# The two MLP down projections computed by seven products of 2x2 blocks instead of eight

## The chip, the cores and the metric

The kernel is one program on one core of a Trainium2 chip. Its time is the device time of one execution in microseconds (us). TensorE (PE) multiplies 128x128 weight tiles with a moving operand and adds into eight PSUM banks; VectorE (DVE), ScalarE (ACT) and GpSimd (POOL) do the elementwise work; SyncE (SP) and others issue DMAs. The tensors are fp32. Products are taken in the fp32r format: an operand x is split into hi (x rounded to fp32r) and lo = x - hi, and a product becomes three matmuls: hi*hi, hi*lo and lo*hi.

## The reference

One inference step of a trunk of two layers on 1024 prompt tokens and 32 sample tokens (8 sequences of 4) with width 1024. Layer 0 has state-space mixers, layer 1 sparse attention. After each mixer stands the MLP, the place of the change; at the end a final RMSNorm.

```python
def sq_relu_mlp(xn, w_up, w_down):     # w_up 1024 x 4096, w_down 4096 x 1024
    h = jax.nn.relu(xn @ w_up)
    return (h * h) @ w_down
...
    hp = hp + sq_relu_mlp(rms_norm(hp, norm_mlp[layer]), w_up[layer], w_down[layer])
    hs = hs + sq_relu_mlp(rms_norm(hs, norm_mlp[layer]), w_up[layer], w_down[layer])
y_prompt = rms_norm(hp, norm_final)
y_sample = rms_norm(hs, norm_final)
```

## The kernel before

Activations lie with features on the partitions and the 1056 tokens along the free axis. Stages follow one another: layer 0's input projection and mixers, its output projection, MLP 0, the attention layer's input projection ("io", token tiles against weights), attention, its output projection, MLP 1 with the final norm.

The up projection of an MLP (`prod`, L1345 on) already uses seven products instead of eight, in Winograd's form: features of the input are taken as pairs of blocks, output features as pairs, tokens as two halves of 528. Weight sums (`sums`, L1310, POOL) and input differences (`b_sum`, L1225, POOL) are split into hi and lo (ACT cast, DVE subtraction: L1321 and L1322 for weights, L1215 and L1216 for inputs) and multiplied as tiles of 128x264 (L1355 to L1357). Each result is squared after relu on DVE (L1337), multiplied by the squared norm scale `r2` on POOL (L1338), and stored to the DRAM tensor `h_d`.

The down projection (`down`, L1391 on, `dense`, L369 on) goes over 8 groups G of 512 hidden features. Per group, four rows of `h_d` are loaded by SP and split (L330, L331), and weights arrive in units of 1024 columns through the shared weight queue (`w_load`, `w_split`: L306, L315, L316), which also prefetches the first units of the next stage. For each of 8 output blocks d and 3 token chunks of 352 there are 4 x 3 matmuls into a bank of four (`mm`); the result is added to Y in SBUF by DVE (L1400). In group 6 the residual is added, in group 7 each finished piece goes to `finish`: for layer 0 the sum of squares, the residual's store, and the hi and lo parts of the attention layer's input (`resid`, L1192 to L1197); for layer 1 the squares and, once a chunk of tokens is complete, the final norm (`norm4`, L2343 on) and the output's store.

What sets the order: a framework derives the semaphores from the tiles and places each engine's instructions by their order in the program, as far as their buffers are free; each engine then runs its queue in order. A tile's tag has a fixed number of buffers: "wh" 4, "w" 2, "h" 8 (of 512 columns), "sw" 3, "x" 5 in the MLP phase (one of them holds `r2`), "s" 25 (of 1056 columns).

Of the kernel before, what the change touches and what calls it, by code (L numbers as in the profile page):

```python
# [7 lines left out]
F32 = mybir.dt.float32  # L8
F32R = mybir.dt.float32r
# [94 lines left out]
def _prep(i):  # L104
# [90 lines left out]
def _build(ctx, nc, tc, ins, outs, dbg):  # L195
# [988 lines left out]
    def resid(d, c, src, g, xn, acc):  # L1184

        cc = slice(c * CH, (c + 1) * CH)
        if d == 0:
# [9 lines left out]
        V.scalar_tensor_tensor(lo, src, g, hi.bitcast(F32), op0=OP.mult, op1=OP.subtract)  # L1197

# [65 lines left out]
    def ob_unit(d):  # L1264
        def evac(c, p):
            a = ACC[d][:, c * CH:(c + 1) * CH]
            t = half(F32, "ot")
            V.tensor_tensor(t[:, :CH], p[:, :CH], rBs[:, c * CH:(c + 1) * CH], OP.mult)
            V.tensor_tensor(a, a, t[:, :CH], OP.add)
            resid_w(d, c, a, g_mlp[:, d:d + 1], WX1, acc1)  # L1270
# [22 lines left out]
    def mlp(l, W, acc, finish):  # L1293

        R, SF, SW = {}, {}, {}
        st = {"u": U_MLP[l], "H": {}, "Y": {}}
# [37 lines left out]
        def act(x, f, j, c):  # L1334
# [3 lines left out]
            nc.gpsimd.tensor_tensor(x, x, st["r2"][:, tok], OP.mult)  # L1338
# [46 lines left out]
        def h_load(G):  # L1385
            for k in range(4):
                t = xslot(F32, "hr")
                nc.sync.dma_start(t[:, :NT], h_d[l][4 * G + k])
                st["H"][k, G] = split1(t, "hh")

        def down(G, d):  # L1391
            def evac(c, p):
                cc = slice(c * CH, (c + 1) * CH)
                if G == 0:
                    if c == 0:
                        st["Y"][d] = slot(F32, "Y")
                    S.copy(st["Y"][d][:, cc], p[:, :CH])
                    return
                y = st["Y"][d]
                V.tensor_tensor(y[:, cc], y[:, cc], p[:, :CH], OP.add)  # L1400
                if G == 7:
                    finish(d, c, y)
                if G == 6:
                    res = half(F32, "res")
                    nc.sync.dma_start(res[:, :CH], res_d[2 * l][d][:, cc])
                    V.tensor_tensor(y[:, cc], y[:, cc], res[:, :CH], OP.add)
                if G == 7 and c == 2:
                    st["Y"][d] = None
            e = d % 2
            u = st["u"]  # L1410
            if e == 1:
                st["u"] += 1
            act = [st["H"][k, G] for k in range(4)]
            return dense(u, act, range(4), evac, off=512 * e, first=(e == 0), last=(e == 1))
# [993 lines left out]
```

## Time and profile before

| | |
|---|---|
| median of three runs | 3175.05 us (3171.71 to 3177.97) |
| the profiled execution | 3170.71 us, span 3168.8 us |
| PE, DVE, ACT, POOL busy in the span | 96%, 66%, 41%, 25% |
| mean granted clock of PE | 0.984 of full speed |
| DMA | 328.55 MB, 104 GB/s in the mean |

The span is what the profiler records between the first and the last instruction; the execution's own time has a little more around it. Busy times are shares of the span. A matmul's busy time is longer than the distance to the next one, since matmuls overlap; the number of matmuls in a stretch that PE fills says how far apart they are.

### The profile page before, as it was taken

Reading aid. Unit: us, or ns where it says so; the run is one execution under the profiler, and the core shown is the slowest. Engines: PE = TensorE matmul, PEld = TensorE weight load, DVE = VectorE, ACT = ScalarE, POOL = GpSimd, SP = SyncE. Lnnn points to the kernel's source line nnn. Section 1 sums busy time; section 2 is a strip of 40 time slices with the busy share of each in tenths; the row PEclk is TensorE's granted clock in tenths of the full one; section 3 lists DMA queues with packets and bytes.
Section 4 is the critical chain, followed back from the end, with each engine's and each line's share of the span. In section 5 each row is a group of like instructions: output and inputs, shape, how many; then the busy total and the mean of one; then the engine's idle time right before and its main releaser. Section 6 shows DMA issues by size and latency. Waiting matters only on the chain. (4 is left out here: it accounts for less than half of the span.)

```text
span 3168.8 us, 55263 instructions
## 1 busy us (share of the span) xinstructions
PE 3037.3 (96%) x21451; PEld 2871.4 (91%) x21451; DVE 2081.9 (66%) x4075; ACT 1290.5 (41%) x2575; POOL 784.0 (25%) x771
## 2 busy tenths in 40 slices
PE   7999998998999999999999989999999999999998
PEld 5999886898999999999999777777778999999998
DVE  4778787788766444466224777878776776644456
ACT  4223666434333321123236666666653333331112
POOL 0000000016666200001001344343333666510000
PEclk8999999999999999999999999999999999999999
DMA  5345453522333532228631122121143233353232
GB/s 185 94 128 156 113 131 120 165 85 94 106 107 106 173 101 96 67 87 247 163 92 57 18 67 59 23 61 41 21 119 118 95 106 109 113 174 99 78 93 80
DMA packets 219852, 328.55 MB, mean 104 GB/s; under 512 B 71283, under 2 KB 164694, under 8 KB 219526
## 3 DMA queue, kind: packets, MB, share of 16 engines
q1 hardware_dynamic: 189760, 264.03, 27.5%
q0 software_dynamic: 17728, 36.77, 4.7%
q10 hardware_dynamic: 12102, 24.22, 2.0%
q8 instruction: 169, 2.77, 0.4%
q14 instruction: 93, 0.76, 0.1%
HBM read 224.30 MB, written 92.22 MB: 100 GB/s over the span
## 5 line engine op out<-in xcount | busy, mean ns | idle before, releaser
L384 PE MATMUL mm<-hh,wh 128*128 128x352 f32 x1440 | 465.1, 323 | 0.2 <-ACT c L1363 0.2
L386 PE MATMUL mm<-hh,wh 128*128 128x352 f32 x1440 | 464.9, 323 | 0.0
L385 PE MATMUL mm<-hh,wh 128*128 128x352 f32 x1440 | 464.5, 323 | 0.0
L1400 DVE TENSOR_TENSOR Y<-Y,mm 128x352 f32<-128x352 f32 x336 | 173.8, 519 | 273.1 <-PE mm L386 272.3
L315 ACT CAST wh<-wr 128x1024 fp32r<-128x1024 f32 (+3 forms) x121 | 122.9, 1016 | 468.8 <-PE mm L385 453.4
L1355 PE MATMUL A<-xw,sw 128*128 128x264 f32 x1024 | 291.7, 286 | 2.3 <-ACT xw L1215 1.6
L1357 PE MATMUL A<-xw,sw 128*128 128x264 f32 x1024 | 292.4, 286 | 1.0 <-DVE sw L1322 1.0
L1356 PE MATMUL A<-xw,sw 128*128 128x264 f32 x1024 | 293.0, 286 | 0.1
L2124 POOL TENSOR_SCALAR P<-P,s,gates 128x640 f32<-128x640 f32 (+7 forms) x256 | 211.9, 841 | 277.1 <-DVE s L2120 229.0
L385 PEld LDWEIGHTS mm<-hh,wh 128*128 128x128 f32 x1440 | 271.2, 188 | 0.0
L384 PEld LDWEIGHTS mm<-hh,wh 128*128 128x128 f32 x1440 | 270.7, 188 | 0.4 <-ACT c L1363 0.4
L386 PEld LDWEIGHTS mm<-hh,wh 128*128 128x128 f32 x1440 | 270.9, 188 | 0.0
L1338 POOL TENSOR_TENSOR e<-e,r 128x264 f32<-128x264 f32 x192 | 196.6, 1030 | 225.1 <-DVE e L1337 221.6
L384 PE MATMUL mm<-xh,wh 128*128 128x352 f32 x672 | 224.5, 335 | 7.0 <-ACT xh L435 5.9
L385 PE MATMUL mm<-xl,wh 128*128 128x352 f32 x672 | 222.5, 331 | 5.2 <-DVE xl L436 5.2
L386 PE MATMUL mm<-xh,wh 128*128 128x352 f32 x672 | 221.7, 330 | 0.0
L2142 DVE TENSOR_TENSOR PT<-px,PT 128x512 fp32r<-128x512 f32 x264 | 176.8, 682 | 51.2 <-ACT PT L2141 50.6
L316 DVE TENSOR_TENSOR wh<-wr,wh 128x1024 fp32r<-128x1024 f32 (+3 forms) x121 | 143.8, 1188 | 100.1 <-ACT wh L315 100.1
L2166 PE MATMUL pv<-PT,vs 128*128 128x512 f32 x528 | 195.3, 438 | 11.6 <-ACT PT L2141 6.8
L2116 ACT ACTIVATE P<-sc,m 128x640 f32<-128x640 f32 (+7 forms) x256 | 180.1, 713 | 41.0 <-DVE m L2110 30.1
L1355 PEld LDWEIGHTS A<-xw,sw 128*128 128x128 f32 x1024 | 193.8, 190 | 2.9 <-ACT xw L1215 1.7
L1357 PEld LDWEIGHTS A<-xw,sw 128*128 128x128 f32 x1024 | 194.1, 190 | 1.4 <-DVE sw L1322 1.4
(631 smaller groups left out, 8305.6 us busy)
## 6 DMA issues: line engine op xcount, KB each, us to landing
hr<-h_d SPq DMA_DIRECT2D x64, 528.0 KB
wu<-i_w_up SPq DMA_DIRECT2D x64, 512.0 KB
wr<-i_w_dn SPq DMA_DIRECT2D x64, 512.0 KB
h_d<-e SPq DMA_DIRECT2D x192, 132.0 KB
wr<-i_w_in_e POOLq DMA_DIRECT2D x26, 512.0 KB, 4.1
h_d<-c SPq DMA_DIRECT2D x64, 132.0 KB
res<-res SPq DMA_DIRECT2D x48, 176.0 KB
csb<-cs_d SPq DMA_DIRECT2D x16, 512.0 KB
```

What stands on the lines that cost most here:

```text
L384: T.matmul(o, wh, xh, start=(j == 0), stop=False)
L385: T.matmul(o, wh, xl, start=False, stop=False)
L386: T.matmul(o, wl, xh, start=False, stop=(j == n - 1))
L1338: nc.gpsimd.tensor_tensor(x, x, st["r2"][:, tok], OP.mult)
L1355: T.matmul(o, a, xh, start=bool(first and q == 0), stop=False, skip_group_check=True)
L1356: T.matmul(o, a, xl, start=False, stop=False, skip_group_check=True)
L1357: T.matmul(o, b, xh, start=False, stop=(q == 3), skip_group_check=True)
L1400: V.tensor_tensor(y[:, cc], y[:, cc], p[:, :CH], OP.add)
L2116: S.activation(P, reg[:, h - h0], AF.Exp, bias=b["m"][:, h:h + 1], accum_out=b["s"][:, h:h + 1])
L2124: nc.gpsimd.tensor_scalar(P, P, b["s"][:, h:h + 1], GT[:, qb, gc:gc + 1], op0=OP.mult, op1=OP.mult)
L2142: V.tensor_tensor(lo, p, hi.bitcast(F32), OP.subtract)
L2166: T.matmul(PV[g, qb, i], v, t, start=(a == 0 and kb == 0 and k == 0), stop=False)
```

## The change

The down projection of both layers takes the hidden features, the output features and the tokens as 2x2 blocks and computes seven products p1 to p7 of blocks or of sums of blocks. In the diff, A are the weights and B the hidden activations: a step q (of 16) takes the pair of hidden rows 2q and 2q+1 and all 4 pairs of output blocks (dp). The products go one after the other (p1, p5, p6, p2, p4, p7, p3), each over all 16 steps, 24 matmuls of 264 columns a step, into all eight PSUM banks (`dn`). For every product the operands are loaded anew by SP (`a_load` 256 KB, `b_load` 264 KB); the sums TR (of B) and SR (of A) stay in SBUF and are altered in place by POOL from product to product (`ready`, `after`). `two_of` is the split. `ready` of a step stands two steps ahead of its matmuls in program order. `evac` adds the products into Y.

The product by `r2` moves from the up stage to the end: `done` takes a piece of 128x264 (32 pieces in all), multiplies it by `r2` (DVE), adds the residual (POOL), and calls `finish`, unless p3 is still to come for it. Two pieces are placed behind each step of p3. In layer 1, p3 is done in two passes over the token quarters (`last`), with its weight sum split already during p7 into `S4`, and the final norm is called between the steps (`hook4`). The prefetch of the first three weight units of the attention layer's input projection is held until MLP 0 is through. `w_dn` is laid out in memory as 64 blocks of 128x512.

```diff
-        a[f"w_dn{l}"] = np.stack([np.concatenate([_unit(wd[G * 512:(G + 1) * 512, d * 128:(d + 1) * 128])
-                                                  for d in (2 * e, 2 * e + 1)], 1) for G in range(8) for e in range(4)])
+        a[f"w_dn{l}"] = np.ascontiguousarray(wd.reshape(16, 2, 128, 4, 2, 128).transpose(4, 1, 0, 2, 3, 5).reshape(64, 128, 512))
...
-        return psum[-1][1].tile([128, 512], F32, name=f"{name}{cnt[0]}", tag="px", bufs={"att": 3, "up": 1}.get(psum[-1][2], 4))
+        return psum[-1][1].tile([128, 512], F32, name=f"{name}{cnt[0]}", tag="px", bufs={"att": 3, "up": 1}.get(psum[-1][2], 4)) if psum[-1][2] != "dn" else dn()
+    def dn():
+        cnt[0] += 1
+        return psum[-1][1].tile([128, 512], F32, name=f"dn{cnt[0]}", tag="dn", bufs=8)
...
-    U_MLP = [len(units), 0]
-    def mlp_units(l):
-        return [(ins[f"w_dn{l}"][j], 1024) for j in range(32)]
-    units += mlp_units(0)
...
-    U_MLP[1] = len(units)
-    units += mlp_units(1)
...
-    held = {U_MLP[l] + i for l in range(2) for i in range(2)}
+    held = {U_IO + i for i in range(3)}
...
+    seen = set()
+    def sq_add(acc, cc, src, key):
+        if (key, cc.start) not in seen:
+            seen.add((key, cc.start))
             S.activation(acc[:, cc], src, AF.Square)
         else:
-            t = half(F32, "sq")[:, :CH]
+            t = half(F32, "sq")[:, :cc.stop - cc.start]
             S.activation(t, src, AF.Square)
             V.tensor_tensor(acc[:, cc], acc[:, cc], t, OP.add)
-        if c == 0:
+    def resid(d, cc, src, g, xn, acc):
+        sq_add(acc, cc, src, "acc2")
+        if d not in xn:
             xn[d] = slot(F32R, "xn"), slot(F32R, "xn")
         hi, lo = (t[:, cc] for t in xn[d])
         S.activation(hi, src, AF.Copy, scale=g)
         V.scalar_tensor_tensor(lo, src, g, hi.bitcast(F32), op0=OP.mult, op1=OP.subtract)
...
-            nc.gpsimd.tensor_tensor(x, x, st["r2"][:, tok], OP.mult)
             nc.sync.dma_start(h_d[l][f][:, tok], x)
...
-        def h_load(G):
...
-        def down(G, d):
...
+        Y, TR, SR, S4, PS = {}, {}, {}, {}, {}
+        def a_load(i, k, q):
+            t = half(F32, "ar")
+            nc.sync.dma_start(t, ins[f"w_dn{l}"][(2 * i + k) * 16 + q])
+            return t
+        def b_load(k, j, q, second=False, o=0, n=HF):
+            t = wslot(F32, "br", "w", 2) if second else ptile(F32, "br", "sw", 3, 1024)
+            nc.sync.dma_start(t[:, :n], h_d[l][2 * q + k][:, j * HF + o:j * HF + o + n])
+            return t[:, :n]
+        def stay(Z, q, n):
+            if q % 2 == 0:
+                Z["t"] = slot(F32, "st")
+            Z[q] = Z["t"][:, q % 2 * n:(q % 2 + 1) * n]
+            return Z[q]
+        def two_of(x, t):
+            n = x.shape[-1]
+            hi, lo = t[:, :n], t[:, n:2 * n]
+            S.copy(hi, x)
+            V.tensor_tensor(lo, x, hi.bitcast(F32), OP.subtract)
+            return hi, lo
+        sub = lambda o, x, y: nc.gpsimd.tensor_tensor(o, x, y, OP.subtract)
+        wt = lambda: wslot(F32R, "sb", "wh", 4)
+        xt_ = lambda: xslot(F32R, "xb")
+        def ready(n, q):
+            if n == "p1":
+                a, x, b12 = a_load(0, 0, q), b_load(0, 0, q), b_load(0, 1, q, True)
+                sub(stay(TR, q, HF), b12, x)
+            elif n == "p5":
+                a21, a22 = a_load(1, 0, q), a_load(1, 1, q)
+                a = stay(SR, q, 512)
+                nc.gpsimd.tensor_tensor(a, a21, a22, OP.add)
+                x = TR[q]
+            elif n == "p6":
+                a, x = SR[q], TR[q]
+                sub(a, a, a_load(0, 0, q))
+            elif n == "p2":
+                a, x = a_load(0, 1, q), b_load(1, 0, q)
+            elif n == "p4":
+                a, b21 = a_load(1, 1, q), b_load(1, 0, q)
+                x = ptile(F32, "t4", "wr", 2, 1024)[:, :HF]
+                sub(x, b21, TR[q])
+            elif n == "p7":
+                a, x = half(F32, "s3"), TR[q]
+                sub(a, a_load(1, 1, q), SR[q])
+            else:
+                a, x = half(F32, "s4"), b_load(1, 1, q)
+                sub(a, a_load(0, 1, q), SR[q])
+            return two_of(a, wt()), two_of(x, xt_())
+        def after(n, q):
+            if n == "p5":
+                sub(TR[q], b_load(1, 1, q), TR[q])
+            elif n == "p4":
+                sub(TR[q], TR[q], b_load(0, 0, q, True))
+            elif n == "p7" and l:
+                sub(SR[q], a_load(0, 1, q), SR[q])
+                S4[q] = two_of(SR[q], slot(F32R, "s4"))
+        tok = lambda j, c: slice(j * HF + c * 264, j * HF + (c + 1) * 264)
+        res_ = lambda d, cc: res_d[2 * l][d][:, cc]
+        def scale_res(d, cc):
+            y, res = Y[d][:, cc], half(F32, "res")[:, :264]
+            nc.sync.dma_start(res, res_(d, cc))
+            V.tensor_tensor(y, y, st["r2"][:, cc], OP.mult)
+            nc.gpsimd.tensor_tensor(y, y, res, OP.add)
+        todo = []
+        def evac(n, dp, c, o):
+            d0, d1 = 2 * dp, 2 * dp + 1
+            if n in ("p1", "p5") and c == 0:
+                Y[d0 if n == "p1" else d1] = slot(F32, "Y")
+            y = lambda i, j: Y[d1 if i else d0][:, tok(j, c)]
+            if n == "p1":
+                S.copy(y(0, 0), o)
+            elif n == "p5":
+                S.copy(y(1, 1), o)
+            elif n == "p6":
+                V.tensor_tensor(y(1, 0), y(0, 0), o, OP.add)
+                nc.gpsimd.tensor_tensor(y(0, 1), y(1, 0), y(1, 1), OP.add)
+            elif n == "p2":
+                V.tensor_tensor(y(0, 0), y(0, 0), o, OP.add)
+                todo.append((d0, 0, c))
+            elif n == "p4":
+                V.tensor_tensor(y(1, 0), y(1, 0), o, OP.add)
+            elif n == "p7":
+                V.tensor_tensor(y(1, 1), y(0, 1), o, OP.add)
+                V.tensor_tensor(y(1, 0), y(1, 0), o, OP.add)
+                todo.extend(((d1, 0, c), (d1, 1, c), (d0, 1, c)))
+            else:
+                t = e_t()
+                V.tensor_tensor(t, o, st["r2"][:, tok(1, c)], OP.mult)
+                V.tensor_tensor(y(0, 1), y(0, 1), t, OP.add)
+                finish(d0, tok(1, c), Y[d0])
+        def done(k):
+            d, j, c = k
+            scale_res(d, tok(j, c))
+            if (d % 2, j) != (0, 1):
+                finish(d, tok(j, c), Y[d])
+        def step(n, q, ops, cs=(0, 1)):
+            (wh, wl), (xh, xl) = ops
+            for dp in range(4):
+                a, b = (t[:, dp * 128:(dp + 1) * 128] for t in (wh, wl))
+                for c in cs:
+                    if q == 0:
+                        PS[dp, c] = dn()[:, :264]
+                    o = PS[dp, c]
+                    h, g = (t[:, c * 264:(c + 1) * 264] if len(cs) == 2 else t for t in (xh, xl))
+                    T.matmul(o, a, h, start=(q == 0), stop=False)
+                    T.matmul(o, a, g, start=False, stop=False)
+                    T.matmul(o, b, h, start=False, stop=(q == 15))
+                    if q == 15:
+                        evac(n, dp, c, o)
+        def down():
+            ks = [(n, q) for n in ("p1", "p5", "p6", "p2", "p4", "p7") + (() if l else ("p3",)) for q in range(16)]
+            ops = {}
+            for i, k in enumerate(ks):
+                if k[0] == "p3" and k[1] == 0:
+                    todo.sort()
+                for z in ([0, 1, 2] if i == 0 else [i + 2]):
+                    if z < len(ks):
+                        ops[z] = ready(*ks[z])
+                step(*k, ops.pop(i))
+                after(*k)
+                if k[0] == "p3":
+                    for _ in range(2):
+                        if todo and (todo[0][0] < 4 or todo[0][0] < 4 + k[1] // 4):
+                            done(todo.pop(0))
+            while todo and not l:
+                done(todo.pop(0))
+        def last():
+            todo.sort(key=lambda k: (k[1], k[2], k[0]))
+            for c in range(2):
+                ops = {}
+                for q in range(16):
+                    for z in ([0, 1, 2] if q == 0 else [q + 2]):
+                        if z < 16:
+                            x = b_load(1, 1, z, z % 2 == 1, c * 264, 264)
+                            ops[z] = S4[z], two_of(x, wt())
+                    step("p3", q, ops.pop(q), (c,))
+                    for _ in range(2):
+                        if todo:
+                            done(todo.pop(0))
+                    hook(c, q)
...
-        held.clear() if l else held.difference_update({U_MLP[0], U_MLP[0] + 1})
-        w_load(st["u"])
-        w_split(st["u"])
-        w_load(st["u"] + 1)
-        h_load(0)
         prod(15, "p3")
         W["x"].clear()
-        new_psum("mlp")
-        for G in range(8):
-            if G < 7:
-                h_load(G + 1)
-            if G == 7:
-
...
+        new_psum("dn")
+        down()
+        if l:
+            last()
...
-    def fin2(d, c, y):
-        resid(d, c, y[:, c * CH:(c + 1) * CH], g_odd[:, d:d + 1], X2, acc2)
-        if c == 2:
-            nc.scalar.dma_start(res_d[1][d], y[:, :NT])
+    def fin2(d, cc, y):
+        resid(d, cc, y[:, cc], g_odd[:, d:d + 1], X2, acc2)
+        nc.scalar.dma_start(res_d[1][d][:, cc], y[:, cc])
     mlp(0, WX1, acc1, fin2)
+    held.clear()
 
...
+    def fin4(d, cc, y):
+        if not YF:
+            YF["acc"] = slot(F32, "acc4")
         YF[d] = y
...
+        sq_add(YF["acc"], cc, y[:, cc], "acc4")
...
+    def norm4(t):
...
+    def hook4(c, q):
+        for t, at in enumerate(((0, 13), (1, 3), (1, 9), (1, 15))):
+            if at == (c, q):
+                norm4(t)
...
-    mlp(1, WX3, acc3, fin4)
+    mlp(1, WX3, acc3, fin4, hook4)
```

## Rows read from the trace of the kernel before

**Rows 1.** the page: busy us (share of the span) xinstructions; GB/s in 40 slices
```profile
PE 3037.3 (96%) x21451; PEld 2871.4 (91%) x21451; DVE 2081.9 (66%) x4075; ACT 1290.5 (41%) x2575; POOL 784.0 (25%) x771
...
GB/s 185 94 128 156 113 131 120 165 85 94 106 107 106 173 101 96 67 87 247 163 92 57 18 67 59 23 61 41 21 119 118 95 106 109 113 174 99 78 93 80
```

**Rows 2.** the page's chain of waits, shares of the span by engine
```profile
PE 35%; DVE 3%; ACT 1%; issue 1%; DMA 0%; SPq 0%; POOL 0%; DVEq 0%; ACTq 0%; POOLq 0%
```

**Rows 3.** stretches: length, busy us of PE, PEld, DVE, ACT, POOL; PEclk, DMA, GB/s
```profile
725.00:1066.36 341.36, 333.33 (x2698) 332.20 (x2698) 250.75 (x362) 127.18 (x265) 220.50 (x189) 0.99 0.35 110
1066.36:1437.30 370.94, 370.79 (x2307) 370.50 (x2306) 184.73 (x289) 90.28 (x126) 5.99 (x5) 1.00 0.32 104
2783.14:3156.50 373.36, 373.36 (x2324) 373.03 (x2322) 184.28 (x294) 80.00 (x108) 4.98 (x5) 1.00 0.30 98
3156.50:3168.80 12.30, 1.84 (x10) 1.40 (x9) 6.57 (x16) 1.46 (x4) 0.00 (x0) 0.62 0.37 130
2441.80:2466.00 24.20, 17.19 (x104) 16.36 (x105) 24.20 (x27) 14.21 (x29) 15.35 (x9) 0.79 0.14 44
```

**Rows 4.** timeline of POOL early in the second up projection: start us, us
```profile
2447.72 1.75 POOL L1310 TENSOR_TENSOR sf<-sf,wu 128x512 f32<-128x512 f32 x1
2449.43 1.76 POOL L1225 TENSOR_TENSOR xa<-xa,xa 128x528 f32<-128x528 f32 x1
2451.15 1.72 POOL L1310 TENSOR_TENSOR sf<-wu,wu 128x512 f32<-128x512 f32 x1
2452.82 3.46 POOL L1225 TENSOR_TENSOR xa<-xa,xa 128x528 f32<-128x528 f32 x2
```

**Rows 5.** timeline of DVE, same stretch and just behind it
```profile
2449.95 1.78 DVE L1322 TENSOR_TENSOR sw<-wu,sw 128x512 fp32r<-128x512 f32 x1
2451.66 1.75 DVE L1322 TENSOR_TENSOR sw<-sf,sw 128x512 fp32r<-128x512 f32 x1
...
2465.21 0.68 DVE L1322 TENSOR_TENSOR sw<-wu,sw 128x512 fp32r<-128x512 f32 x1
2465.81 0.69 DVE L1216 TENSOR_TENSOR xw<-xa,xw 128x528 fp32r<-128x528 f32 x1
2466.43 0.42 DVE L1337 SCALAR_TENSOR_TENSOR e<-e 128x264 f32<-128x264 f32 x1
2466.78 0.69 DVE L1216 TENSOR_TENSOR xw<-xa,xw 128x528 fp32r<-128x528 f32 x1
```

**Rows 6.** timeline of POOL, middle of the first up projection
```profile
859.30 1.28 POOL L1310 TENSOR_TENSOR sf<-wu,sf 128x512 f32<-128x512 f32 x1
...
861.98 1.19 POOL L1338 TENSOR_TENSOR c<-c,r 128x264 f32<-128x264 f32 x1
863.13 1.75 POOL L1310 TENSOR_TENSOR sf<-sf,wu 128x512 f32<-128x512 f32 x1
```

**Rows 7.** groups of DVE by shape: xcount, busy us, mean ns, idle before
```profile
L1367 DVE TENSOR_TENSOR e<-e,C 128x264 f32<-128x264 f32 x64 | 27.0, 425 | 12.2 <-PE C L1357 12.1
L2360 DVE SCALAR_TENSOR_TENSOR Y<-Y,p_norm_final,px 128x352 f32<-128x352 f32 x24 | 12.1, 575 | 2.0 <-PE px L2357 2.0
```

**Rows 8.** a group of ACT by shape
```profile
L1321 ACT CAST sw<-sf 128x512 fp32r<-128x512 f32 x128 | 79.5, 622 | 117.9 <-POOL sf L1310 57.4 <-PE B L1357 53.5 <-PE C L1357 3.8
```

**Rows 9.** stretches of other stages, columns as in rows 3
```profile
500.00:600.00 100.00, 89.55 (x593) 74.63 (x592) 81.09 (x157) 51.01 (x94) 3.23 (x6) 0.93 0.48 156
1437.30:1480.00 42.70, 42.09 (x343) 41.46 (x342) 33.15 (x103) 14.96 (x29) 9.81 (x9) 0.96 1.03 315
1445.00:1455.00 10.00, 10.00 (x74) 9.97 (x74) 5.46 (x35) 3.03 (x7) 3.35 (x3) 0.83 1.07 386
1800.00:1900.00 100.00, 88.44 (x663) 74.53 (x661) 70.82 (x147) 59.69 (x163) 43.97 (x60) 0.98 0.25 58
```

**Rows 10.** SP: the weight loads of the next stage, and one load's issue (ns)
```profile
1394.93 38.76 SPq L306 DMA_DIRECT2D wr<-i_w_io  x3
L1388 SPq DMA_DIRECT2D hr<-h_d x64: 319/326/1847, 1046.7 to 3017.5; - x64
```

More of the change, by code (lines that the diff above doesn't have):

```diff
@@ L1197, in resid, with ob_unit, evac @@
         V.scalar_tensor_tensor(lo, src, g, hi.bitcast(F32), op0=OP.mult, op1=OP.subtract)
+    def ob_unit(d):
+        def evac(c, p):
+            a = ACC[d][:, c * CH:(c + 1) * CH]
+            t = half(F32, "ot")
+            V.tensor_tensor(t[:, :CH], p[:, :CH], rBs[:, c * CH:(c + 1) * CH], OP.mult)
+            V.tensor_tensor(a, a, t[:, :CH], OP.add)
+            resid_w(d, c, a, g_mlp[:, d:d + 1], WX1, acc1)
+            if c == 2:
+                nc.scalar.dma_start(res_d[0][d], ACC[d][:, :NT])
+                ACC[d] = None
+        return dense(U_OB + d, YH, range(8), evac)
     HF = NT // 2
@@ L1262, in _build @@
     acc1 = ptile(F32, "acc1", "big", 2, 1152)
[L1264 to L1270, printed above, removed]
-            if c == 2:
-                nc.scalar.dma_start(res_d[0][d], ACC[d][:, :NT])
-                ACC[d] = None
-        return dense(U_OB + d, YH, range(8), evac)
     for d in range(8):
@@ L1383, in prod @@
                 prep(p + 1, ORDER.index(wn))
-        def h_load(G):
[L1386 to L1389, printed above, removed]
-        def down(G, d):
[L1392 to L1400, printed above, removed]
-                if G == 7:
[L1402 to L1414, printed above, removed]
@@ L2325, in _build @@
     YF = {}
-    acc4 = slot(F32, "acc4")
-    def fin4(d, c, y):
+    def fin4(d, cc, y):
+        if not YF:
+            YF["acc"] = slot(F32, "acc4")
         YF[d] = y
-        cc = slice(c * CH, (c + 1) * CH)
-        if d == 0:
-            S.activation(acc4[:, cc], y[:, cc], AF.Square)
-        else:
-            t = half(F32, "sq")[:, :CH]
-            S.activation(t, y[:, cc], AF.Square)
-            V.tensor_tensor(acc4[:, cc], acc4[:, cc], t, OP.add)
-        for k, at in enumerate(((2, 1), (2, 2), (7, 2))):
-            if at == (d, c):
-                norm4(k)
-    r4 = const("rf", [128, 9])
-    def norm4(c):
+        sq_add(YF["acc"], cc, y[:, cc], "acc4")
+    r4 = const("rf", [128, 12])
+    V.memset(r4, 1.0)
+    def norm4(t):
         p = px()
-        n = [min(128, CH - i * 128) for i in range(3)]
+        o, n = t * 264, (128, 128, 8)
         for i in range(3):
-            o = c * CH + i * 128
-            T.matmul(p[:n[i], i:i + 1], acc4[:, o:o + n[i]], C["ones"][:, 0:1], start=True, stop=True)
-        r = r4[:, 3 * c:3 * c + 3]
-        V.memset(r, 1.0)
+            T.matmul(p[:n[i], i:i + 1], YF["acc"][:, o + i * 128:o + i * 128 + n[i]], C["ones"][:, 0:1], start=True, stop=True)
+        r = r4[:, 3 * t:3 * t + 3]
         V.tensor_scalar(r[:, :2], p[:, :2], 1.0 / D, EPS, op0=OP.mult, op1=OP.add)
@@ L2357, in norm4 @@
             T.transpose(p[:, i * 128:(i + 1) * 128], r[:, i:i + 1].to_broadcast([128, 128]), ident)
-        cc = slice(c * CH, (c + 1) * CH)
+        cc = slice(o, o + 264)
         for k in range(8):
-            V.scalar_tensor_tensor(YF[k][:, cc], YF[k][:, cc], g_fin[:, k:k + 1], p[:, :CH], op0=OP.mult, op1=OP.mult)
+            V.scalar_tensor_tensor(YF[k][:, cc], YF[k][:, cc], g_fin[:, k:k + 1], p[:, :264], op0=OP.mult, op1=OP.mult)
             nc.sync.dma_start(outs["yT"][k][:, cc], YF[k][:, cc])
+    def hook4(c, q):
+        for t, at in enumerate(((0, 13), (1, 3), (1, 9), (1, 15))):
+            if at == (c, q):
+                norm4(t)
     WX3["raw"] = up_raw(1, 0)
```

18 lines of the change are left out of this document (2 added, 16 removed).

## The prediction

> **What bounds the kernel now.** First the busy times: PE is busy for 96% of the span, DVE for 66%, POOL for 25% [rows 1], and in the chain of waits PE holds by far the largest share of those named [rows 2]. A mean over stages doesn't say what a stage can bear, so next the stretches [rows 3]: the first down projection lasts 370.9 us and PE is busy in all of it at full granted clock (2.4 GHz), while DVE works half of it and POOL almost nothing; the second is the same. So there time is matmuls times their spacing. The up projections, which already use seven products, are as full of matmuls, but DVE and POOL are busy about 73% and 65% of the time. That is the stage which the new one will resemble, so the next look is at how DVE and POOL bear each other.
>
> They don't run beside each other when both read two operands from SBUF. At the start of the second up projection both have work queued: the POOL instructions (512 and 528 columns) start 1.71 us apart [rows 4], and so do the DVE subtractions [rows 5]: one pair every 1.71 us. When POOL is silent, the same DVE subtractions start 0.60 to 0.62 us apart, those of 264 columns 0.35 us [rows 5]. So DVE's share of a pair is 0.61 and POOL's 1.10 us; they take turns. For 264 columns on POOL: two starts are 1.15 us apart with one DVE subtraction of 512 between [rows 6], so 0.54. PE lost 24.2 - 17.2 = 7 us in that stretch [rows 3]. DVE additions that read PSUM keep 0.425 us in the middle of this traffic [rows 7], so they are free of it. I call the time in which either holds the second operand's way "port time".
>
> **The change, part by part.**
>
> *Matmuls.* Before: 8 groups x 8 feature blocks x 3 x 12 = 2304 per layer in 370.9 us: 0.161 us each. After: 7 products x 16 steps x 24 = 2688 of 264 columns; the up stage shows that shape at 333.3/2698 = 0.1235 us [rows 3], so 332.0 us a layer. The two stages took 370.9 + 373.4 = 744.3; with 2.4 us kept for the final norm's own PE work the saving is 744.3 - 663.9 - 2.4 = 78.0 us, if PE never waits. The Trainium skill ("TensorE: Matmul & The Clock Gate", section "Wait — 56ns, not 53.3ns?") has warm matmuls start N/2.4 ns + 2.5 ns apart: 112.5 and 149.2 ns here, about 11 ns under the rows; by it the saving would be an estimated 82.7 before the norm. The sum goes by the rows. One step is 24 x 0.1235 = 2.96 us of PE, a product 47.4.
>
> *What a step asks of the port.* Each step has two splits (DVE 0.61 each) and a number of POOL sums (1.10 each): p1, p6: 2.32 us; p2: 1.22; p5 and p4 (two sums): 3.42; p7 in layer 0: 2.32, in layer 1 (two sums, and the third split for S4): 4.03. Against 2.96 for PE. The four "wh" buffers let operands be up to three steps ahead, 8.9 us. p5 lacks 0.46 x 16 = 7.4, which the lead covers, and p6 restores it; p4 lacks the same, covered by what p2 restores. Between nothing and that 7.4 I take 1 us each: p5 2, p4 of layer 0 1. In layer 1 p7 follows p4 at once and lacks 1.07 x 16 = 17.1 more: 24.5 - 8.9 = **15.6 us**. ACT casts at 0.62 us [rows 8] stay under PE's step.
>
> *p3 of layer 0.* Two splits and a sum: 2.32. Beside them two pending pieces a step: a piece is y*r2 (0.35), the residual on POOL (0.54), and for three in four the square's addition and the low half of the next input (2 x 0.35): 1.42 in the mean. A step is 2.32 + 2.83 = 5.15. Before the last split come 16 x 2.32 + 26 x 1.415 = 73.9 us of port time; less three steps made ahead (7.0), plus PE's last step and latency 3.7, it is 70.6 against 47.4: **+23.2 us**. To put the pieces behind the splits would not help: the next stage needs all of them. Before, the same finishing lay under the last group with POOL silent.
>
> *From layer 0 to the next stage.* After the last split 6 pieces (8.5) and eight evacuations of 0.42 + 3 x 0.35 (11.8) remain: 20.3 us. PE still has 3.7 us, and three token tiles of 24 matmuls (2.9 each at 0.123, the 343 matmuls in 42.1 us [rows 3, 9]) before the norm needs everything: idle 8 us. The weights of that stage were fetched early, their three loads issued from 1394.9 on [rows 10]; now they are released only after the layer and come amid traffic of 315 GB/s [rows 9], so 3 to 16, I take **8**. Two evacuations per bank at the end of p7 (16 x 0.425 = 6.8 us for 8 banks, PE's slack 4.9): 2.
>
> *p3 of layer 1.* Its two passes have 12 matmuls a step, 1.48 us. In the first pass a step has a split of 264 (0.35) and two pieces of 0.35 + 0.54 + 3/4 x 0.35 = 1.15: 2.65. 1.17 x 16 = 18.7, less what lies ahead: **18 us**. The second pass has the norm only.
>
> *Rest.* The product by r2 leaves the up stage: 256 POOL instructions, under PE's work there, gain nothing. Each down stage's start: 1 us. The tail after the last matmul was 12.3 us [rows 3]; its eight scalings are 264 instead of 352 columns wide (0.575 us [rows 7]): -1. DMA: p1 wants 784 KB in 2.96 us, 265 GB/s; the trace shows 386 GB/s over 10 us and 315 over 43 [rows 9], and an SP issue takes 0.33 us [rows 10], three a step. I put it at nothing; if landings come late, see the fourth rival.
>
> *Unfilled port time.* 246 us are now set by the port (p4 and p7 of layer 1 120, p3 of layer 0 84, the last pass 42). At the start of an up stage it goes without a gap [rows 4]: 0. If instead each instruction's parts outside the port added up, a pair would cost 1.28 (POOL's shortest of 512 columns, [rows 6]) + 0.68 [rows 5] = 1.96, 15% more: 37 us. I take 12, nearer to the stretch without gaps.
>
> *Sum.* -78 + 15.6 + 23.2 + 18 + 8 + 2 + 3 + 2 - 1 + 12 = **+4.8 us**. The profiled execution took 3170.7 us (span 3168.8), the median of the runs shown is 3175.05, 4.3 more. So 3175.5 on the profiled one's scale, 3180 as a median: no change that can be told, or a little slower.
>
> **The rivals.**
> 1. PE sets the pace everywhere: DVE and POOL hide. By DVE alone p3 of layer 0 needs 2.97 us a step and the last pass 1.57, as much as PE. Then -78 + 2 + 8 + 2 + 1 - 1 + 4 = -62: 3113. For it: the up stage is full at 65 and 73%. Against it: [rows 4, 5].
> 2. The finishing in layer 1 slides into the second pass, whose port is free: both passes need 48 us of port time against 47.4 of PE. Then the 18 and 7 of the unfilled time go: 3155. Against it: the pieces stand before the next split in program order, and DVE is in order.
> 3. Slower: the clock. PE is busy 73% in p7 of layer 1 and 57% in p3 of layer 0. Over 100 us with PE at 90% the granted clock was 0.93 [rows 9], and in the stretch where it waited (71% busy) 0.79 [rows 3]. At the lower level (1.2 GHz) a step is 5.9 us, over the port's 4.03 and 5.15: 1.9 x 16 + 0.8 x 16 = 43 us if it stays there, half that if it goes to and fro: 3201. It decides once PE's clock is under 0.75 in p7 of layer 1. The Trainium skill ("TensorE: Matmul & The Clock Gate", section "HAM oscillation — how this bites in real kernels") describes such a kernel, whose PE is throttled anew by each wait for data; the trace agrees only in part: the attention stage, with PE busy 88% and waiting in short pieces, has 0.98 [rows 9].
> 4. Slower: transfers. p1's second operand and p4's late one have two buffers; were the loads held to 247 GB/s, the best slice of the 40 [rows 1], a step would take 3.17 us in p1, p5 and p4: 0.21 x 16 x 6 = +20: 3200.
>
> **How the numbers follow.** Forecast 0.45; rivals 0.15, 0.20, 0.12, 0.08. The forecast's own range is 3158 to 3214 (unfilled time 0 to 37, the transition 3 to 16, leads off by 5 in two places). Within 0.2% (6.4 us) a measurement can't tell it from no change. Faster: 0.15 + 0.18 of the second rival + 0.10 of the forecast = 0.43; same: 0.02 + 0.13 = 0.15; slower: 0.22 + 0.20 = 0.42. The range 3128 to 3214 leaves out the first rival and the ends.
>
> **What would show it.** In the profile after: matmuls of 264 columns in the down stages 0.1235 us apart wherever PE doesn't wait. p1, p5, p6, p2 near 47 to 49 us each; p7 of layer 1 near 63, with p4 near 47 to 49 ahead of it; p3 of layer 0 near 71; the first pass of p3 in layer 1 near 42, the second near 24. PE's waits in the long ones name DVE splits, and POOL's and DVE's instructions there are stretched, not idle. A gap of 8 us before the token tiles. It is wrong if p3 of layer 0 takes under 55 us, or if p1 is already well over 50, or if waits name DMA.

## The result, and the profile after

The changed kernel takes 3228.31 us (median of 4 runs, 3223.03 to 3231.60) beside 3176.51 us for the kernel before: ratio 1.0157, 95% interval 1.0127 to 1.0186. It is slower by 52 us, 48 above the forecast and 14 above the end of the range. The profiled execution took 3228.73 us, span 3226.9.

The page of the changed kernel, busy times and the chain of waits, against [rows 1, 2]:

```profile
PE 3006.0 (93%) x22228; PEld 2819.0 (87%) x22228; DVE 2285.6 (71%) x4234; ACT 1414.7 (44%) x2920; POOL 1011.6 (31%) x851
...
PE 26%; DVE 8%; DMA 2%; POOL 2%; ACT 2%; issue 2%; SPq 0%; DVEq 0%; ACTq 0%; POOLq 0%
```

PE holds 26% of the chain where it held 35%, and its busy time fell by 31 us only: it now waits. Where, the stretches say (columns as in [rows 3]): p1, p5, p6, p2, p4, p7, p3 of layer 0; the second up projection; p4, p7 and the two passes of p3 of layer 1; the tail.

```profile
1079.32:1129.13 49.81, 49.22 (x385) 48.64 (x386) 33.01 (x37) 22.51 (x40) 26.45 (x18) 0.97 0.89 310
1129.13:1181.91 52.78, 49.55 (x387) 47.42 (x385) 52.52 (x31) 22.11 (x44) 52.78 (x32) 1.00 0.76 236
1181.91:1233.91 52.00, 48.95 (x387) 48.53 (x386) 40.80 (x40) 18.95 (x34) 27.44 (x18) 0.97 0.37 106
1233.91:1280.81 46.90, 46.90 (x386) 46.90 (x385) 29.48 (x40) 18.50 (x32) 16.29 (x13) 1.00 0.62 199
1280.81:1339.15 58.34, 50.33 (x387) 47.61 (x385) 52.10 (x47) 19.33 (x34) 51.85 (x33) 1.00 0.66 193
1339.15:1388.41 49.26, 48.76 (x384) 48.55 (x385) 37.50 (x48) 18.89 (x34) 22.54 (x17) 0.97 0.38 107
1388.41:1459.55 71.14, 53.71 (x386) 51.76 (x384) 63.95 (x98) 31.92 (x64) 41.49 (x37) 0.90 0.54 161
...
2478.20:2824.87 346.67, 337.25 (x2698) 335.31 (x2698) 217.60 (x358) 122.15 (x261) 95.88 (x67) 0.98 0.29 97
...
3025.40:3087.40 62.00, 50.59 (x385) 47.59 (x384) 56.62 (x50) 19.90 (x35) 56.27 (x35) 0.98 0.61 182
3087.40:3144.80 57.40, 51.87 (x384) 50.80 (x385) 53.19 (x56) 23.17 (x44) 39.45 (x25) 0.93 0.35 106
3144.80:3174.70 29.90, 25.55 (x204) 24.45 (x202) 24.14 (x67) 10.98 (x28) 13.85 (x10) 1.00 0.40 114
3174.70:3201.20 26.50, 24.73 (x204) 24.28 (x201) 20.40 (x49) 8.46 (x23) 11.78 (x13) 1.00 0.59 181
3201.20:3226.87 25.67, 4.24 (x21) 3.12 (x19) 16.57 (x41) 4.61 (x14) 6.29 (x8) 0.57 0.44 143
```

In p2 PE, with 46.9 us, does what was forecast. In p5 POOL is never idle (52.78 of 52.78) and in p4 it is busy for 51.85 of 58.34 us, while in p6 it works half of the time and in p2 a third: the work is unevenly spread, and the idle half does not come back. The tail is twice as long as in [rows 3].

The 58 us between the two profiled spans, cut at the first and last matmul of each stage (the cuts are good to 0.3 us):

| stretch | before | after | difference |
|---|---|---|---|
| up to the first up projection | 725.5 | 732.3 | +6.9 |
| up projections 0 and 1 | 340.8, 341.2 | 345.4, 346.0 | +9.4 |
| down 0 and 1, with the gap ahead | 370.8, 373.5 | 381.9, 377.0 | +14.5 |
| layer 0's end to the second up projection | 1004.8 | 1018.7 | +13.9 |
| tail | 12.3 | 25.7 | +13.4 |

### The profile page after: what moved, and what is told of

The parts are those of the page before. It is cut to its first block, busy times and chain, and to the rows that moved or that the text cites. A ratio compares the mean times of both kernels' runs of the same rounds, so it can differ in the third digit from the quotient of the medians.

```text
span 3226.9 us, 58490 instructions
## 1 busy us (share of the span) xinstructions
PE 3006.0 (93%) x22228; PEld 2819.0 (87%) x22228; DVE 2285.6 (71%) x4234; ACT 1414.7 (44%) x2920; POOL 1011.6 (31%) x851
## 5 line engine op out<-in xcount | busy, mean ns | idle before, releaser
L1510 PE MATMUL dn<-xb,sb 128*128 128x264 f32 x1664 | 477.0, 292 | 30.2 <-DVE xb L1411 30.2
L1509 PE MATMUL dn<-xb,sb 128*128 128x264 f32 x1664 | 455.0, 290 | 23.5 <-ACT sb L1410 10.4
L1511 PE MATMUL dn<-xb,sb 128*128 128x264 f32 x1664 | 461.2, 288 | 5.1 <-DVE sb L1411 5.1
L1510 PEld LDWEIGHTS dn<-xb,sb 128*128 128x128 f32 x1664 | 319.0, 192 | 39.1 <-DVE xb L1411 39.1
L1509 PEld LDWEIGHTS dn<-xb,sb 128*128 128x128 f32 x1664 | 309.7, 193 | 28.3 <-ACT sb L1410 12.0
L1511 PEld LDWEIGHTS dn<-xb,sb 128*128 128x128 f32 x1664 | 316.2, 193 | 7.0 <-DVE sb L1411 7.0
L2260 DVE TENSOR_TENSOR PT<-px,PT 128x512 fp32r<-128x512 f32 x264 | 177.0, 683 | 50.7 <-ACT PT L2259 49.8
L1359 PEld LDWEIGHTS A<-xw,sw 128*128 128x128 f32 x1024 | 195.9, 191 | 2.2 <-DVE sw L1325 2.2
L1357 PEld LDWEIGHTS A<-xw,sw 128*128 128x128 f32 x1024 | 195.0, 191 | 2.4 <-ACT xw L1230 1.3
L1358 PEld LDWEIGHTS A<-xw,sw 128*128 128x128 f32 x1024 | 195.6, 191 | 0.9 <-DVE xw L1231 0.9
L2259 ACT CAST PT<-px 128x512 fp32r<-128x512 f32 x264 | 152.3, 593 | 98.6 <-PE px L2270 97.6
L2214 PE MATMUL sc<-KT,qt 128*128 128x256 f32 x1216 | 191.3, 296 | 0.0
L1325 DVE TENSOR_TENSOR sw<-sf,sw 128x512 fp32r<-128x512 f32 x128 | 110.9, 868 | 112.5 <-ACT sw L1324 112.4
```

The lines of the kernel that those rows point to most:

```text
L1357: T.matmul(o, a, xh, start=bool(first and q == 0), stop=False, skip_group_check=True)
L1358: T.matmul(o, a, xl, start=False, stop=False, skip_group_check=True)
L1359: T.matmul(o, b, xh, start=False, stop=(q == 3), skip_group_check=True)
L1509: T.matmul(o, a, h, start=(q == 0), stop=False)
L1510: T.matmul(o, a, g, start=False, stop=False)
L1511: T.matmul(o, b, h, start=False, stop=(q == 15))
```

## The experiments

Ratios are to the kernel before on the same chip; stage times are of the profiled execution.

**All sums of the down stages on DVE.**

```diff
-        sub = lambda o, x, y: nc.gpsimd.tensor_tensor(o, x, y, OP.subtract)
+        sub = lambda o, x, y: V.tensor_tensor(o, x, y, OP.subtract)
...
-            nc.gpsimd.tensor_tensor(y, y, res, OP.add)
+            V.tensor_tensor(y, y, res, OP.add)
```

> All sums of the down stages, the residual's addition among them, on DVE; POOL has none there. Turn-taking: a sum is 0.61 us on DVE against 1.10 on POOL, and the other engine can't work meanwhile anyway, so every step gets shorter: p5 and p4 4 x 0.61 = 2.44 a step, under PE's 2.93, so 47 us each (now 52.8 to 62); p7 of layer 1 5 x 0.61 = 3.05, 49 (57.4); p3 of layer 0 about 59 (71.1); the tail shorter by 4. Sum near -60 us against the changed kernel, 3165 to 3180. Rival (DVE and POOL do work side by side, and late loads are what PE waits for): DVE only gets more to do, nothing is gained in p5, p4 and p7, and p3 of layer 0 gets longer: 3230 or more.

3176.66 us, ratio 1.0009 (0.9999 to 1.0019). p5, p6, p2 and p4 take 46.9 us each in both layers, p7 47.3: the turn-taking was the cause there. What was missed lies behind them: p3 of layer 0 rose to 79.9, the first pass of layer 1 to 32.3, and the tail stayed at 25.3. POOL is silent in p3, so taking turns with it does not set it; the waits of that stretch (who waits for whom: us in total, times, longest) name a circle of ACT and DVE queues instead:

```profile
PE dn L1509 <- ACT sb L1410: 18.4, 8, 3.8
ACT sq L1190 <- DVE Y L1462: 12.9, 11, 3.3
ACT sb L1410 <- DVE s L1414: 11.3, 9, 1.7
```

The cast that PE needs stands in ACT's queue behind the square of a piece, which waits for DVE's residual sum. The granted clock in these 79.9 us was 0.83; how much of them that makes, no run shows.

**Block sums of 16 columns.** `sub` on POOL takes 16 columns only, on operands loaded in place; the sums of the rest are left out.

> Leaves out the block sums but for 16 of their columns; loads, splits, matmuls and the finishing stay. Turn-taking: p5, p6, p4 and p7 fall to 47 or 48 us each in both layers (from 52.8, 52.0, 58.3, 49.3 and 53.0, 52.0, 62.1, 57.4), p3 of layer 0 to about 56 by its finishing (from 71): near -70, 3155. Late loads: the same loads come, so the products keep their times within 3 us.

3158.44 us, ratio 0.9947 (0.9927 to 0.9967). All products but p1 (49.2, 47.7) and p3 take 46.9. p3 of layer 0 still takes 61.6 (about 56 expected), the passes 29.2 and 26.6, the tail 25.5: what is left lies where the finishing does.

**No residual loads.**

```diff
-            y, res = Y[d][:, cc], half(F32, "res")[:, :264]
-            nc.sync.dma_start(res, res_(d, cc))
+            y, res = Y[d][:, cc], st["r2"][:, cc]
```

> Leaves out the residual's loads in the finishing; POOL adds a slice of the norm scale instead, at the same price. Turn-taking alone: p3 of layer 0 stays within 5 us of 71, the tail after the last matmul of 25 falls only by its DMA wait of 5. Late loads and a blocked SP queue: p3 of layer 0 under 60, the gap before the next stage down by 8 or more, the tail under 17.

3222.99 us, ratio 1.0158 (1.0134 to 1.0183). The tail falls to about what it was before. The way from layer 0's end to the next up projection falls by 5 us, which is no more than it varies by itself (see the kernel before, once more). p3 of layer 0 stays at 71.8. Its tail, beside the last line of the stretches above:

```profile
3211.40:3224.65 13.25, 1.83 (x12) 1.16 (x10) 7.28 (x21) 1.89 (x5) 0.00 (x0) 0.69 0.33 112
```

The total hardly moves, as the stretch up to the first up projection took 737.2 us, p4 of layer 0 64.3 (58.3 in the changed kernel), and p4 + p7 and the first pass of layer 1 123.8 and 34.9 (119.4 and 29.9). Why p4 and what follows took more here stays open.

**Only the residual's sum on DVE** (the second line of the first diff alone).

> Only the residual's addition moves from POOL to DVE. Turn-taking: 0.54 - 0.35 = 0.19 us for each of 32 pieces a layer, 6 us a layer, and two hand-overs a piece go: -12 to -20 us in p3 of layer 0, the last passes and the tail; p5, p4, p7 as they are. Side by side: DVE gets 0.35 more per piece, p3 of layer 0 +11.

3235.46 us, ratio 1.0198 (1.0175 to 1.0220): nothing is gained; p3 of layer 0 71.8, passes 32.7 and 26.6.

**The kernel before, once more.**

> The kernel before, unchanged, profiled a second time. The changed kernel's profile has 17 us more ahead of the down stages than the one profile of before: +6.9 us before the first up stage starts (725.4 against 732.3, same order of PE instructions) and +4.6 and +4.9 us in the up stages (340.8 and 341.2 against 345.4 and 346.0). Theory A, it is the timing of the half-clock stretches, which differs from execution to execution: then this second profile has another split, the start of the first up stage anywhere in 725 to 733 and up stages anywhere in 341 to 346, with the span 3169 to 3185. Rival B, it belongs to the change (its instruction streams differ): then this profile repeats 725 +-1 and 341 +-1, as every profile of the changed kernel's family gave 343.4 to 346.5.

3177.02 us, span 3175.2. Its stretch up to the first up projection, then the two up projections:

```profile
0.00:735.00 735.00, 689.36 (x4523) 630.90 (x4524) 563.43 (x1235) 327.44 (x596) 36.08 (x52) 0.95 0.43 129
735.00:1075.80 340.80, 334.10 (x2697) 332.96 (x2698) 250.03 (x359) 126.37 (x264) 220.50 (x189) 0.98 0.35 109
2447.56:2788.80 341.24, 335.37 (x2697) 334.45 (x2698) 251.28 (x359) 127.07 (x265) 221.17 (x190) 0.98 0.35 110
```

Both theories hold, each for one part. The start varies from execution to execution (725.5 and 735.0 us for the same kernel; over all eleven profiles 725 to 737), with a granted clock of 0.97 and 0.95: the +6.9 can't be put down to the change. The up projections repeat to 0.1 us, so their difference can. The way from layer 0's end to the second up projection varies as well: 1000.2 us here, 1004.8 in the first profile of the same kernel.

**The product by r2 back in the up projection.**

```diff
+            nc.gpsimd.tensor_tensor(x, x, st["r2"][:, tok], OP.mult)
             nc.sync.dma_start(h_d[l][f][:, tok], x)
...
-            V.tensor_tensor(y, y, st["r2"][:, cc], OP.mult)
```

> The changed kernel with the product by r2 back in the up stages, where the kernel before has it (POOL, 264 columns), and out of the finishing. Step of the prediction: the product under PE's work in the up stage gains nothing by leaving; it lies on DVE's path in the finishing, 0.35 us a piece. If so: up stages as now (345 to 346), p3 of layer 0 71.1 - 26 x 0.35 = 62 us, the first pass of layer 1 30 to 27, the tail and the transition 1 to 3 us shorter, total 3210 to 3220. Rival 1: the up stages change (to 341, as in the kernel before, or by several us the other way), which would make the place of this product the cause of the 5 us in each. Rival 2: the late loads set the finishing's pace, not DVE: p3 of layer 0 stays at 69 to 72, total 3225 to 3232.

3213.37 us, ratio 1.0132 (1.0112 to 1.0152). Up projections 340.6 and 340.9: the first rival holds, too. p3 of layer 0 64.6, first pass 24.5 (the piece is shorter on DVE), the tail still 25.8; the way from layer 0's end to the next up projection took 1023.8, which was not expected. Why more work on POOL makes the up projection shorter is seen in the timelines (start us, us) of POOL and DVE at its start. The changed kernel, whose stage starts at 2478.2, POOL and then DVE:

```profile
2492.61 3.49 POOL L1240 TENSOR_TENSOR xa<-xa 128x528 f32<-128x528 f32 x2
2496.06 1.74 POOL L1313 TENSOR_TENSOR sf<-wu,sf 128x512 f32<-128x512 f32 x1
2497.76 1.73 POOL L1313 TENSOR_TENSOR sf<-wu 128x512 f32<-128x512 f32 x1
2499.57 1.63 POOL L1313 TENSOR_TENSOR sf<-sf,wu 128x512 f32<-128x512 f32 x1
```

```profile
2498.27 4.11 DVE L1231 TENSOR_TENSOR xw<-xa,xw 128x528 fp32r<-128x528 f32 x3
```

and this experiment, whose stage starts 5.0 us earlier:

```profile
2487.54 3.50 POOL L1240 TENSOR_TENSOR xa<-xa 128x528 f32<-128x528 f32 x2
2498.31 5.06 POOL L1341 TENSOR_TENSOR e<-e,r 128x264 f32<-128x264 f32 x2 [7.27 <-DVE e L1340]
```

```profile
2489.78 3.69 DVE L1231 TENSOR_TENSOR xw<-xa,xw 128x528 fp32r<-128x528 f32 x4
```

Here POOL's queue stops for 7.3 us at the first product by `r2`, and DVE splits four inputs in 3.69 us. Without that product POOL goes on to the weight sums of the next pair, and three splits take 4.11; counted from the start of the stage, the four input splits and the weight split among them are done 3.3 us later. In the first 40 us PE does 191 matmuls and not 230, which at 0.122 us each is 4.8 us; the rest of the stage is alike. Most of it is lost in the last 16.2 of these 40 us, here of the changed kernel and of this experiment (columns as in [rows 3]):

```profile
2502.00:2518.20 16.20, 14.00 (x96) 13.39 (x97) 13.62 (x27) 7.81 (x16) 2.31 (x1) 0.89 0.10 34
```

```profile
2496.96:2513.16 16.20, 15.97 (x131) 15.76 (x130) 15.45 (x27) 7.07 (x15) 11.45 (x8) 1.00 0.19 53
```

PE waits more there, and its granted clock is 0.89 and not 1.00. That the product's place makes the difference is shown by the run; the way it does so is read from these views, and how much of the 4.8 us is wait and how much clock stays open.

**Sums on DVE, the finishing early.** As the first experiment, with the product by `r2` in the up projection; residuals loaded on POOL's queue and added behind the steps of p2, for the block whose p5 part is already in y01 through `y11 = y01 + res`; the remaining pieces spread by hand over p7 and p3, and p4 and the first pass.

```diff
+            res = half(F32, "res")[:, :264]
+            nc.gpsimd.dma_start(res, res_(d, cc))
+            V.tensor_tensor(y, Y[2 * dp][:, cc] if ij == 2 else y, res, OP.add)
...
-                V.tensor_tensor(y(1, 1), y(0, 1), o, OP.add)
+                V.tensor_tensor(y(1, 1), y(1, 1), o, OP.add)
...
+                if k[0] == "p2":
+                    res_add(2 * k[1])
+                    res_add(2 * k[1] + 1)
+                for t in (LATE if l else EARLY).get(k, ()):
+                    todo.remove(t)
+                    done(t)
```

> A version that should beat both: block sums on DVE as in the first experiment; the product by r2 back on POOL in the up stages (256 instructions of 264 columns); the residuals loaded on POOL's queue and added on DVE during p2, before they are needed; the pieces of the finishing that are left are squares, sums of squares and low halves, spread over p7 and p3 (layer 0) and p4 and the first pass (layer 1). My theory (the loss is turn-taking of POOL and DVE plus the finishing and its loads lying late): p1 to p7 46.9 to 48 each in both layers, p3 of layer 0 47 to 53 (DVE needs 2.7 us a step of 2.93), the end of the layer to the next up stage 1010 to 1016, first pass 24 to 27, second 23.5 to 26, tail 12 to 16; down stages 333 to 338 and 330 to 336; total 3115 to 3130. Rival (PE's waits come from something else in the finishing, for example ACT's casts waiting in line or the landing of loads): p3 of layer 0 stays at 60 or more, as with the small sums (61.6), the tail at 25, total 3150 or more.

3108.60 us, ratio 0.9805 (0.9788 to 0.9821): 2% below the kernel before, under the range expected. Stretches p5, p4 and p3 of layer 0, the two passes and the tail:

```profile
1120.51:1167.36 46.85, 46.85 (x387) 46.85 (x386) 46.83 (x77) 21.07 (x42) 2.21 (x4) 1.00 0.95 334
...
1262.15:1309.06 46.91, 46.91 (x384) 46.91 (x385) 43.60 (x75) 20.50 (x36) 0.00 (x0) 1.00 0.85 273
...
1355.95:1406.31 50.36, 47.31 (x385) 46.88 (x384) 44.80 (x95) 30.53 (x66) 0.00 (x0) 1.00 0.66 206
...
3040.07:3065.13 25.06, 24.48 (x204) 24.26 (x202) 17.16 (x50) 11.49 (x30) 0.00 (x0) 1.00 0.36 104
3065.13:3090.35 25.22, 25.22 (x209) 25.13 (x210) 17.13 (x50) 8.07 (x22) 0.00 (x0) 1.00 0.45 140
3090.35:3102.28 11.93, 1.86 (x12) 1.20 (x10) 5.96 (x18) 1.48 (x5) 0.00 (x0) 0.63 0.40 136
```

The down projections take 332.7 and 334.1 us, as the prediction's 332.0 for PE alone; layer 0's end to the next up projection takes 1005.5.

**The same with the block sums on POOL.**

```diff
-        sub = lambda o, x, y: V.tensor_tensor(o, x, y, OP.subtract)
+        sub = lambda o, x, y: nc.gpsimd.tensor_tensor(o, x, y, OP.subtract)
...
-                V.tensor_tensor(a, a21, a22, OP.add)
+                nc.gpsimd.tensor_tensor(a, a21, a22, OP.add)
...
-                V.tensor_tensor(y(0, 1), y(1, 0), y(1, 1), OP.add)
+                nc.gpsimd.tensor_tensor(y(0, 1), y(1, 0), y(1, 1), OP.add)
```

> The improved version with the block sums back on POOL, as in the changed kernel: the fourth corner of sums on POOL or DVE by finishing late or early (early: r2 in the up stage, residuals added on DVE in p2, pieces spread). Theory (two separate causes, whose prices add): what the sums cost in p5, p6, p4 and p7 comes back, p5 52 to 54, p6 52 to 56, p4 54 to 60, p4 + p7 of layer 1 113 to 119, while p3 of layer 0 stays near 50 to 57 (port 2.32 + 20/16 x 0.70 = 3.2 us a step against 2.93), the passes near 25 and the tail near 12: total 3150 to 3170. Rival (one cause: the late finishing makes the turn-taking harmful, without it the lead covers it, as the prediction had it): the products 46.9 to 49, total 3108 to 3125.

3179.59 us, ratio 1.0025 (1.0012 to 1.0038). p5 53.1, p6 55.1, p4 58.1, p4 + p7 of layer 1 119.1; p3 of layer 0 52.0, passes 25.1 and 25.3, tail 11.9. Two causes, then. With the sums on POOL, the finishing early rather than late is worth 34 us (3213.4, the sixth experiment, to 3179.6): the place of the pieces, the residual's sum on DVE and its loads on POOL's queue together, which no run takes apart. With it early, the sums on DVE are worth 71 more. The total is 9.6 us over the range expected; 6.5 of them lie in p2, at 50.5 and 49.8, where POOL adds Y and issues the residuals' loads.

**Operands made three steps ahead in the program**, `i + 3` for `i + 2`.

> The changed kernel with operands made three steps ahead in program order, not two; buffers as they are. It tests the step of the prediction that a lead of three steps (8.9 us) covers what p5 and p4 lack. Theory A (the lead was only cut short by the order of the program, two steps): p5 47 to 50, p6 47 to 50, p4 of layer 0 50 to 54 and p4 + p7 of layer 1 10 us shorter, total 3200 to 3212. Rival B (the lead is not there to be had: in p1 the operands come as the loads land, POOL waits for each of them, and in p6 and p2 POOL takes the sums of the next product into the time that should rebuild it): p5 51 to 54, p6 50 to 56, p4 57 to 62, total 3222 to 3235.

3224.89 us, ratio 1.0172 (1.0142 to 1.0201): no difference from the changed kernel. p5 51.9 and 53.6, p6 50.9 and 52.9, p4 58.7 and 61.1.

## Why the prediction was wrong, point by point

**Spacing of the matmuls: right.** 0.122 us where PE does not wait, 46.9 us a product against 47.4. With the sums on DVE and the finishing early, where nothing else stands in its way, the two down projections take 77.5 us less than before (666.8 against 744.3).

**Price of the port: right.** At p5's end POOL and DVE start in turn, as in [rows 4, 5], with no gap:

```profile
1169.81 1.73 POOL L1426 TENSOR_TENSOR st<-ar,ar 128x512 f32<-128x512 f32 x1
1171.50 6.87 POOL L1414 TENSOR_TENSOR st<-st,ar 128x512 f32<-128x512 f32 x4
1178.33 3.53 POOL L1414 TENSOR_TENSOR st<-br,st 128x528 f32<-128x528 f32 x2
1181.83 3.41 POOL L1414 TENSOR_TENSOR st<-st,ar 128x512 f32<-128x512 f32 x2
```

```profile
1172.03 1.78 DVE L1411 TENSOR_TENSOR sb<-st,sb 128x512 fp32r<-128x512 f32 x1
1173.73 1.79 DVE L1411 TENSOR_TENSOR xb<-st,xb 128x528 fp32r<-128x528 f32 x1
1175.45 1.77 DVE L1411 TENSOR_TENSOR sb<-st,sb 128x512 fp32r<-128x512 f32 x1
```

A pair costs 1.72 us, and the last nine steps of p5 take 3.41 to 3.62 by the trace, 3.42 by the sum. The price of 264 columns on DVE, 0.35 us, was read from a relu square in [rows 5] and not from a subtraction; it holds (in the first experiment a residual's sum takes 0.34 or 0.35 us to the next start). The Trainium skill ("SBUF — State Buffer", section "🔬 SBUF: two separate sides") says that the port pair of DVE and GpSimd is locked for a whole instruction and not shared; these rows agree. The 12 us for unfilled port time were not needed in p5.

**The lead of three steps: wrong, the largest error.** The step said that p5 loses nothing to speak of, since a lead of 8.9 us covers the 7.4 that it lacks, and that p6 and p2 restore it. p5 and p6 took 4.4 to 4.6 us more than forecast, each and in both layers, p4 of layer 0 9.9, p4 + p7 of layer 1 8.1; with p1 (+1.6), p2 (-1.0) and p7 of layer 0 (+0.9) that is 37.6 us. In layer 1 the loss was also put in the wrong product: p4 was to take 47 to 49 us and p7 63, and they took 62.0 and 57.4. Two things stood against it. The lead was about one step: after a first step of 4.1 us p5 ran six at 2.93 and then nine at 3.41 to 3.62, so 6 x 0.49 = 2.9 us of lead were used up. In p1 the sums come as the loads land; POOL waited for them 13 times, 26.3 us in total, so little was stored up. And in the timeline above POOL makes four sums of p6 (`st<-st,ar`) ahead of two of p5 (`st<-br,st`). So the deficit of p5 grows by p6's sums, p6's first step takes 7.4 us, and from its third step on PE sets the pace and POOL is half idle. In p4 the sums of p7 come in the same way; three sums and two splits make 4.5 us, and its last four steps take 4.1, 4.7, 4.7 and 7.4:

```profile
1326.31 1.30 POOL L1414 TENSOR_TENSOR st<-st,br 128x528 f32<-128x528 f32 x1
1327.58 1.75 POOL L1414 TENSOR_TENSOR s<-ar,st 128x512 f32<-128x512 f32 x1
1329.30 1.77 POOL L1414 TENSOR_TENSOR t<-br,st 128x528 f32<-128x528 f32 x1
1331.02 1.31 POOL L1414 TENSOR_TENSOR st<-st,br 128x528 f32<-128x528 f32 x1
```

The first two experiments show that the sums on POOL cost this, the last that a longer look-ahead in the program does not give it back. In the eighth p5 takes as long (53.1) but loses most of it in its first step (8.2 us), so where the loss falls is not settled by the price of a step. That the order of POOL's queue and not its total is to blame is read from the timelines; no run changes that order and leaves the rest.

**p3 of layer 0: the number right, the reason only in part.** 71.1 against 70.6, which is in part luck: the account has steps of 5.15 us throughout, and they were uneven (11.3, 8.3 and 6.9 us among others of 2.9 to 4.5); and with POOL silent it took longer, 79.9. With fewer and cheaper pieces in p3, in the eighth experiment, the port account comes out: 3.2 x 16 = 51 expected, 52.0 measured. In the changed kernel the queues of the finishing have a part in it as well; how the 71 divide stays open.

**The passes of layer 1, the transition and the tail: half the second rival, and a load left out.** The passes took 56.4 us instead of 65.4, so 9.0 less, on the way to that rival's 48 (its price is off as well: it takes back 7 us of unfilled time, where the pass's share of the 12 is 12 x 42 / 246 = 2). But the pieces did not only slide from the first pass into the second; they slid past the end. The tail was to fall by 1 us and rose by 13.4. The waits after the last matmuls:

```profile
PE dn L2459 <- DVE acc L1191: 9.9, 1, 9.9
ACT acc L1187 <- POOL Y L1462: 6.4, 1, 6.4
POOL Y L1462 <- DMA res<-res: 5.4, 1, 5.4
```

and behind layer 0 (1459.5 to 1500), where the forecast had a gap of 8 and 13.9 us came:

```profile
POOL Y L1462 <- DMA res<-res: 21.8, 4, 13.5
ACT sq L1190 <- POOL Y L1462: 13.6, 4, 7.2
DVE acc L1191 <- ACT sq L1190: 8.6, 2, 5.3
```

PE waits for DVE, DVE for ACT, ACT for POOL, POOL for a load. The prediction counted a piece by its port time and left out the load at its head. Its issue stands in SP's queue behind operand loads that wait for a buffer (10.7 us in the two passes of layer 1, for DVE's splits), and at the end behind the stores of the output (`o_yT`), which wait for the final norm on DVE (3.0 us before the first of these):

```profile
3196.66 1.80 SPq L2470 DMA_DIRECT2D o_yT<-Y  x4
3198.55 3.34 SPq L1460 DMA_DIRECT2D res<-res  x4
3201.99 1.87 SPq L2470 DMA_DIRECT2D o_yT<-Y  x4
3203.95 3.44 SPq L1460 DMA_DIRECT2D res<-res  x4
```

The last four residuals are loaded behind the last matmul of p3, at 3201.2. The third experiment shows it for the tail: without these loads it is 13.3. For the transition it is not shown, since the 5 us gained there are within what that stretch varies by, and the granted clock in its first 40 us was 0.83 (0.96 before). Waits that name a DMA were among the prediction's own signs of being wrong.

**The product by r2 gains nothing by leaving: wrong.** Its leaving cost 9.4 us in the up projections. Over all profiles, the twelve up projections without it took 343.4 to 346.5 us, the ten with it 340.6 to 341.2.

**Clock and transfers: not the cause in the products.** The granted clock was 1.00 in p5 and p4 of layer 0, and in p7 of layer 1 0.93, far from the 0.75 of the third rival; in p3 of layer 0 it was 0.90, and what that cost is not parted from the waits. p1 moves 310 GB/s in 49.8 us, above the 247 of the fourth rival. (p1's demand was put too low: 784 KB here are 803 thousand bytes, 271 and not 265 GB/s.) The time of the first rival, PE setting the pace (3113), was reached only by another kernel, at 3108.6, where the sums had left POOL and the finishing lay early.

**The sum.** Forecast +4.8 on the spans, measured +58.0: 53.2 are missing. The lead 37.6, p3 of layer 0 0.5, the passes -9.0, the transition 5.9, the tail 14.4, the up projections 9.4, the start, which varies by itself, 6.9, unfilled port time -12: 53.7. Against the second profile of the kernel before, the transition would be 4.6 more and the start 9.6 less.

## What to carry to other kernels

Where two engines take turns at a resource, reckon the demand product by product and not over the stage: a later surplus pays nothing back unless operands are stored ahead of it, and here about one step was. Put both kinds of work on the faster of the two engines before counting on the second (two-operand fp32 sums of 512 columns, taken in turn: 0.61 us on DVE, 1.10 on POOL). What finishes a stage is a chain of queues with a load at its head; load it and add it in the stage's idle middle, and only then cost it by busy time.

## What the runs showed that was not expected

An instruction taken off an engine that is not the bottleneck made the stage longer (345.4 for 340.8 us). By the timelines it had held back later work of its queue, which then took the port from the splits that PE waits for.

The same kernel needs 725.5 or 735.0 us up to its first up projection in two executions, at a granted clock of 0.97 and 0.95 there. A difference of several us between two profiles in a part that the change does not touch is not to be explained by the change; a second profile of before tells.
